# Forgetting attention: head-pair scores by full 128-row matmuls with zero-padded keys, and the decay added by VectorE

## The chip, the cores and the metric

One core of one Trainium2 chip runs the whole program. The metric is device microseconds (us) of one execution, the median of several runs. The engines are named as in the profile: PE (TensorE matmul), PEld (TensorE weight load), DVE (VectorE), ACT (ScalarE), POOL (GpSimd) and SP (SyncE, which issues all DMAs of this kernel). Each engine works through its own instructions in order and waits at semaphores for the others.

## The reference, cut to what matters

A decoder trunk of two layers on 256 tokens of width 1024 (`D_MODEL`), in float32. Layer 0 has a forgetting-attention (FoX) mixer with 16 heads of width 64, layer 1 a latent-attention mixer; each layer also has two SwiGLU half steps and a gated per-layer embedding, with a LayerNorm after each. The change is in the FoX mixer alone:

```python
def fox_mixer(x, w_in, b_f, w_o):
    # logit[t,s] = q_t.k_s/sqrt(d) + sum_{s<j<=t} log f_j
    h = x @ w_in                       # q | k | v | forget-gate logits
    ...
    cum = jnp.cumsum(jax.nn.log_sigmoid(f_logit), axis=1).transpose(0, 2, 1)
    scale = FOX_HEAD_DIM ** -0.5
    def scores(start):                 # 128 queries from start on
        ...
        s = jnp.einsum('bhqd,bkhd->bhqk', qb, k).astype(jnp.float32) * scale
        return s + cb[:, :, :, None] - cum[:, :, None, :]
    o = causal_block_attention(scores, v)   # causal mask, softmax, times v
    return o.reshape(B, S, D_MODEL) @ w_o
```

The term `cb` is the same for all keys of a query, so the softmax doesn't depend on it.

## The kernel before

Every float32 operand of a matmul is split into a high and a low part (`parts`: ACT copies the high part, DVE subtracts it for the low part), and a product is three matmuls: high x high, high x low, low x high (`mm3`). Weights stream in by SP's queue into three raw buffers; `Stream` splits each into high and low (line 163 or 171 on ACT, 164 or 175 on DVE) in one of its slots. When a split is put into the program is decided by a planner, from the durations that `S.busy(...)` and `self.mm` declare; PE's order is the program's order.

The FoX mixer (`fox`) runs: `V` (values of both token blocks), with the forget gates between (`gates`; its small steps s1 to s6 are taken from the queue `bg`, one at each use of a weight and at two places in `ws`), then a loop over eight pairs of heads, j = 0 to 7. In the loop PE does, in this order: `gen_k(j+1)` (24 matmuls of 256 columns), `T(j-1)` (six transposes of the probabilities of the pair before), `QK(j)` (scores of this pair), `gen_q(j+1)` (24 matmuls), `AV(j-1)` (three matmuls of 512 and three of 256 columns). `softmax(j)` stands behind `QK(j)`: DVE adds the causal mask and finds the maximum of each row (line 957), two small operations on each head take the query's own decay out of and back into the row's offset (lines 964 and 965), ACT takes the exponential and its sum (969), DVE the reciprocal (976), and POOL multiplies (979). A pair's probabilities are first needed in the next round of the loop, by `T`.

A pair's 128 rows of `qk` hold two heads of 64 rows. `QK` therefore works with 64 rows at a time: for each head one matmul of 384 columns adds the keys' decay (`negc`, the cumulated log gates times -8 in three parts, chosen by the selector `sel`), and six matmuls of 128 or 256 columns add the product, 14 matmuls for a pair. `gates_transpose` (two transposes by PE and a copy) makes `cq`, the decay by query, just ahead of `QK(0)`.

Of the kernel before, what the change touches and what calls it, by code (L numbers as in the profile page):

```python
# [381 lines left out]
class Trunk:  # L382
    def __init__(self, nc, pools, a, S, rec):
        self.nc, self.a, self.S = nc, a, S
        self.sb, self.ps = pools
        self.rec = rec
        self.bg = deque()
        self.setup()
# [418 lines left out]
    def fox(self, li):  # L807
# [27 lines left out]
        sel = self.tl([128, 16], F32R, "sel", 1)  # L835
        negc = self.tl([128, 384], F32R, "negc", 1)
        cq = self.tl([128, 16, 2], F32, "cq", 1)
# [5 lines left out]
        nc.gpsimd.memset(negc.bitcast(F32), 0.0)  # L843
        sf = fs[:, 1792:1808]
        nc.gpsimd.tensor_tensor(sf, self.ident[:, 16:32], self.ident[:, 48:64], op=ALU.add)
        nc.gpsimd.tensor_tensor(sf, sf, self.ident[:, 80:96], op=ALU.add)
        nc.gpsimd.tensor_tensor(sel, sf, self.ident[:, 112:128], op=ALU.add)
# [5 lines left out]
        def gates():  # L853
# [26 lines left out]
            def s4():  # L880
                nc.scalar.activation(negc[fr, 0:128], m8[:, 0:128], AF.Copy)
                nc.scalar.activation(negc[fr, 128:384], m8, AF.Copy)

            def s5():
                nc.vector.tensor_tensor(
                    negc[64:96, 128:384], m8, negc[fr, 128:384].bitcast(F32), op=ALU.subtract
                )
                nc.vector.tensor_copy(negc[64:96, 0:128], negc[64:96, 128:256].bitcast(F32))
                self.S.busy(dve=400)

            def s6():
                nc.vector.tensor_copy(negc[0:64, :], negc[64:128, :].bitcast(F32))

            rest = lambda: None
            self.bg.extend((s1, rest, rest, s2, rest, rest, s3, rest, s4, s5, s6))

        def gates_transpose():
            tr = self.bank("tr")
            for t in range(2):
                self.transpose(tr[:, 128 * t : 128 * t + 128], sc[:, 128 * t : 128 * t + 128])  # L900
            nc.vector.tensor_copy(
                cq.rearrange("p h t -> p t h"),
                tr[:, 0:256].rearrange("p (t c) -> p t c", c=128)[:, :, 112:128],
            )
# [8 lines left out]
        qk = self.own([128, 2, 2, 512], F32R, "qk")  # L913
        OT = [self.own([128, 4, 2, 256], F32R, tag) for tag in ("ota", "otb")]

        def gen(j, key, c0, at={}, hold=False):
# [534 lines left out]
```

## Time and profile before

| | |
|---|---|
| time before, median of 3 runs | 1101.17 us (1100.28 to 1101.95) |
| span of the profiled execution, first to last instruction | 1100.3 us |
| PE busy (matmul) | 1080.1 us, 98% of the span |
| DVE busy | 711.5 us, 65% |
| ACT busy | 542.5 us, 49% |
| POOL busy | 79.7 us, 7% |
| instructions | 17702 |

The profiled execution has no time of its own in the record beside its span; the span is as long as the fastest of the three runs. Matmuls overlap each other, so the busy time of one matmul is longer than the time until the next one starts: what a group of matmuls costs is read from the start of its first to the start of the next group. In a timeline each row is: start, time, engine, line, operation, what it writes and reads, shapes, count, and in brackets the idle time of the engine before it with what ended it.

### The profile page before, as it was taken

Reading aid. Unit: us, or ns where it says so; the run is one execution under the profiler, and the core shown is the slowest. Engines: PE = TensorE matmul, PEld = TensorE weight load, DVE = VectorE, ACT = ScalarE, POOL = GpSimd, SP = SyncE. Lnnn points to the kernel's source line nnn. Section 1 sums busy time; section 2 is a strip of 40 time slices with the busy share of each in tenths; the row PEclk is TensorE's granted clock in tenths of the full one; section 3 lists DMA queues with packets and bytes.
Section 4 is the critical chain, followed back from the end, with each engine's and each line's share of the span. In section 5 each row is a group of like instructions: output and inputs, shape, how many; then the busy total and the mean of one; then the engine's idle time right before and its main releaser. Section 6 shows DMA issues by size and latency. Waiting matters only on the chain. (4 is left out here: it accounts for less than half of the span.)

```text
span 1100.3 us, 17702 instructions
## 1 busy us (share of the span) xinstructions
PE 1080.1 (98%) x7186; PEld 976.7 (89%) x7186; DVE 711.5 (65%) x1006; ACT 542.5 (49%) x790; POOL 79.7 (7%) x130
## 2 busy tenths in 40 slices
PE   9999999999999999999999999998999999999997
PEld 6989998899879899997899999987899789898986
DVE  5765545788896555458975453487766885454576
ACT  5554433567645534434655353345655474445421
POOL 0000000313100000001320000011111000000000
PEclk9999999999999999999999999999999999999998
DMA  8896652553458756445677564353533678555502
GB/s 280 282 294 223 214 185 72 162 165 135 145 170 279 253 198 191 154 163 163 187 259 245 190 193 143 104 150 107 162 111 111 215 245 276 177 187 175 182 8 77
DMA packets 150676, 199.00 MB, mean 181 GB/s; under 512 B 11842, under 2 KB 128578, under 8 KB 150596
## 3 DMA queue, kind: packets, MB, share of 16 engines
q1 hardware_dynamic: 150596, 197.88, 55.6%
q8 instruction: 56, 0.92, 0.3%
q14 instruction: 24, 0.20, 0.1%
HBM read 196.81 MB, written 1.05 MB: 180 GB/s over the span
## 5 line engine op out<-in xcount | busy, mean ns | idle before, releaser
L164 DVE TENSOR_TENSOR hl<-raw,hl 128x1024 fp32r<-128x1024 f32 (+3 forms) x287 | 334.5, 1184 | 172.5 <-ACT hl L163 171.7
L163 ACT ACTIVATE hl<-raw 128x1024 fp32r<-128x1024 f32 (+3 forms) x287 | 286.9, 1021 | 198.6 <-PE y L469 82.2
L469 PE MATMUL h<-xT,hl 128*128 128x256 f32 x2016 | 239.9, 278 | 1.7 <-DVE P L613 0.7
L469 PEld LDWEIGHTS h<-xT,hl 128*128 128x128 f32 x2016 | 234.1, 188 | 3.7 <-DVE P L613 0.9
L469 PE MATMUL y<-hl,g 128*128 128x512 f32 x816 | 189.6, 390 | 0.0
L469 PEld LDWEIGHTS y<-hl,g 128*128 128x128 f32 x816 | 152.2, 188 | 31.0
L469 PE MATMUL tr<-xT,hl 128*128 128x256 f32 x864 | 102.0, 277 | 0.0
L469 PEld LDWEIGHTS tr<-xT,hl 128*128 128x128 f32 x864 | 100.0, 188 | 0.1
L469 PE MATMUL h<-hl,xT 128*128 128x512 f32 (+1 forms) x396 | 94.7, 388 | 0.4 <-DVE hl L164 0.3
L469 PEld LDWEIGHTS h<-hl,xT 128*128 128x128 f32 x396 | 72.1, 188 | 17.1 <-DVE hl L164 2.2
L541 POOL TENSOR_TENSOR rs<-ve,mhalf 128x1 f32<-128x1 f32 x16 | 15.2, 951 | 827.1 <-DVE ve L540 827.1
L469 PE MATMUL y<-hl,xT 128*128 128x512 f32 (+2 forms) x312 | 61.0, 351 | 0.0
L469 PEld LDWEIGHTS y<-hl,xT 128*128 128x128 f32 x312 | 50.8, 188 | 7.9 <-issue 0.7
L478 ACT ACTIVATE xT<-tr 128x512 fp32r<-128x512 f32 x36 | 20.2, 597 | 58.9 <-PE tr L473 58.9
L479 DVE TENSOR_TENSOR g<-P,g 128x512 fp32r<-128x512 f32 x36 | 24.9, 693 | 34.5 <-ACT g L478 34.5
L478 ACT ACTIVATE g<-P 128x512 fp32r<-128x512 f32 x36 | 22.8, 634 | 40.3 <-DVE P L648 29.4
L164 DVE TENSOR_TENSOR otb<-raw,otb 128x1024 fp32r<-128x1024 f32 (+1 forms) x20 | 24.1, 1203 | 18.9 <-ACT otb L163 18.9
L469 PE MATMUL y<-hl,ota 128*128 128x512 f32 x144 | 36.0, 393 | 0.0
L164 DVE TENSOR_TENSOR qk<-raw,qk 128x1024 fp32r<-128x1024 f32 x21 | 25.8, 1230 | 14.4 <-ACT qk L163 14.4
L469 PE MATMUL tr<-xT,qk 128*128 128x256 f32 x264 | 31.9, 277 | 0.0
L479 DVE TENSOR_TENSOR xT<-tr,xT 128x512 fp32r<-128x512 f32 x36 | 23.3, 683 | 13.3 <-ACT xT L478 13.3
L469 PEld LDWEIGHTS tr<-xT,qk 128*128 128x128 f32 x264 | 30.9, 188 | 0.0
(232 smaller groups left out, 1371.0 us busy)
## 6 DMA issues: line engine op xcount, KB each, us to landing
raw<-in_ffn_w_in_dram SPq DMA_DIRECT2D x172, 512.0 KB, 4.9
raw<-in_ffn_w_out_dram SPq DMA_DIRECT2D x44, 1024.0 KB, 5.1
raw<-in_fox_w_in_dram SPq DMA_DIRECT2D x12, 1024.0 KB, 5.3
raw<-in_ple_w_gate_dram SPq DMA_DIRECT2D x8, 1024.0 KB, 5.0
raw<-in_mla_w_o_dram SPq DMA_DIRECT2D x8, 1024.0 KB, 6.0
gb<-in_ln_g_dram SPq DMA_DIRECT2D x8, 512.0 KB, 6.3
gb<-in_ln_b_dram SPq DMA_DIRECT2D x8, 512.0 KB, 7.4
raw<-in_fox_w_o_dram SPq DMA_DIRECT2D x4, 1024.0 KB, 5.1
```

Of the source, the lines that this page charges most:

```text
L163: nc.scalar.activation(hi[:, c], src[:, c], AF.Copy)
L164: nc.vector.tensor_tensor(lo[:, c], src[:, c], hi[:, c].bitcast(F32), op=ALU.subtract)
L469: self.nc.tensor.matmul(out, lhsT, rhs, start=start, stop=stop)
L478: self.nc.scalar.activation(hi, src, AF.Copy)
L479: self.nc.vector.tensor_tensor(lo, src, hi.bitcast(F32), op=ALU.subtract)
L541: nc.gpsimd.tensor_tensor(rs, ve, self.mhalf, op=ALU.pow)
```

## The change

The scores of a pair become six matmuls over all 128 rows. The keys are kept twice as wide, in `kz`: columns 0 to 255 hold the first head's keys in rows 0 to 63 and zeros below, columns 256 to 511 the second head's in rows 64 to 127 and zeros above, so that a product with the pair's 128 rows of queries (`qq`) gives one head in each half. One bank holds both heads' scores of the first 128 queries (3 matmuls of 2 x 128 columns), the other those of the last 128 (3 of 512 columns). The zeros are written once by POOL.

The decay is no longer added by PE: step s4 stores the 16 rows of `m8` into a DRAM tile, and `load_bias(j)` loads the pair's two rows back, spread over 128 partitions, by two DMAs on SP's queue (128 x 2 x 128 and 128 x 2 x 256 elements); `mask_bias(j)` cuts the causal mask into them on POOL. DVE's line-957 operation then adds `bias` instead of `mask`. `sel`, `negc`, `cq`, `gates_transpose`, steps s5 and s6 and the two small operations on `tt` go. `gen_k` writes its high and low parts in two halves of 64 rows. One reciprocal serves both heads, and the deferred split (`S.later`) stands ahead of it.

```diff
@@ -832,19 +832,17 @@
 
         fs = self.own([128, 2048], F32, "fs")
         bf = self.tl([128, 1], F32, "bf", 1)
-        sel = self.tl([128, 16], F32R, "sel", 1)
-        negc = self.tl([128, 384], F32R, "negc", 1)
-        cq = self.tl([128, 16, 2], F32, "cq", 1)
+        bias = self.tl([128, 2, 2, 384], F32, "fbias", 1)
+        decay = self.dram.tile([16, 256], F32, name="decay")
+        kz = self.own([128, 2, 2, 512], F32R, "qk")
+        qq = self.tl([128, 2, 2, 256], F32R, "qq", 1)
         fr = slice(96, 128)
         nc.gpsimd.memset(bf, 0.0)
         if not self.rec:
             self.dma(bf[112:128, :], a["fox_b_f"][0].rearrange("(p o) -> p o", o=1))
         nc.gpsimd.memset(fs, 0.0)
-        nc.gpsimd.memset(negc.bitcast(F32), 0.0)
-        sf = fs[:, 1792:1808]
-        nc.gpsimd.tensor_tensor(sf, self.ident[:, 16:32], self.ident[:, 48:64], op=ALU.add)
-        nc.gpsimd.tensor_tensor(sf, sf, self.ident[:, 80:96], op=ALU.add)
-        nc.gpsimd.tensor_tensor(sel, sf, self.ident[:, 112:128], op=ALU.add)
+        nc.gpsimd.memset(kz[64:128, :, :, 0:256].bitcast(F32), 0.0)
+        nc.gpsimd.memset(kz[0:64, :, :, 256:512].bitcast(F32), 0.0)
 
         f, e, u, r, ab = (fs[fr, 256 * i : 256 * i + 256] for i in range(5))
         sc = fs[:, 1280:1536]
@@ -878,30 +876,29 @@
                 self.S.busy(dve=600)
 
             def s4():
-                nc.scalar.activation(negc[fr, 0:128], m8[:, 0:128], AF.Copy)
-                nc.scalar.activation(negc[fr, 128:384], m8, AF.Copy)
-
-            def s5():
-                nc.vector.tensor_tensor(
-                    negc[64:96, 128:384], m8, negc[fr, 128:384].bitcast(F32), op=ALU.subtract
-                )
-                nc.vector.tensor_copy(negc[64:96, 0:128], negc[64:96, 128:256].bitcast(F32))
-                self.S.busy(dve=400)
-
-            def s6():
-                nc.vector.tensor_copy(negc[0:64, :], negc[64:128, :].bitcast(F32))
+                self.dma(decay, m8[16:32, :])
+                for j in range(2):
+                    load_bias(j)
+                mask_bias(0)
 
             rest = lambda: None
-            self.bg.extend((s1, rest, rest, s2, rest, rest, s3, rest, s4, s5, s6))
-
-        def gates_transpose():
-            tr = self.bank("tr")
-            for t in range(2):
-                self.transpose(tr[:, 128 * t : 128 * t + 128], sc[:, 128 * t : 128 * t + 128])
-            nc.vector.tensor_copy(
-                cq.rearrange("p h t -> p t h"),
-                tr[:, 0:256].rearrange("p (t c) -> p t c", c=128)[:, :, 112:128],
-            )
+            self.bg.extend((s1, rest, rest, s2, rest, rest, s3, s4))
+
+        def load_bias(j):
+            b = bias[:, j % 2]
+            for c0, w in ((0, 128), (128, 256)):
+                if not self.rec:
+                    d = decay[2 * j : 2 * j + 2, 0:w]
+                    src = bass.AP(tensor=d.tensor, offset=d.offset, ap=[[0, 128], [256, 2], [1, w]])
+                    self.dma(b[:, :, c0 : c0 + w], src)
+
+        def mask_bias(j):
+            b = bias[:, j % 2]
+            for c0 in (0, 256):
+                nc.gpsimd.affine_select(
+                    out=b[:, :, c0 : c0 + 128], in_=b[:, :, c0 : c0 + 128],
+                    pattern=[[0, 2], [-1, 128]], compare_op=ALU.is_ge, fill=NEG, base=0, channel_multiplier=1,
+                )
 
         V(0, 0)
         V(1, 0, VAT, lambda: self.XT(1))
@@ -910,79 +907,73 @@
         V(1, 1)
 
         st, PT = {}, {}
-        qk = self.own([128, 2, 2, 512], F32R, "qk")
         OT = [self.own([128, 4, 2, 256], F32R, tag) for tag in ("ota", "otb")]
 
-        def gen(j, key, c0, at={}, hold=False):
+        def gen_k(j):
             ps = self.bank("h")
-            ws((key, j), ps[:, 0:256], at, hold)
-            o = qk[:, j % 2]
-            self.parts(o[:, 0, c0 : c0 + 256], o[:, 1, c0 : c0 + 256], ps[:, 0:256])
-
-        def gen_k(j):
-            gen(j, "fk", 256, {0: S.split_now} if j >= 2 else {}, j >= 2)
+            ws(("fk", j), ps[:, 0:256], {0: S.split_now} if j >= 2 else {}, j >= 2)
+            o = kz[:, j % 2]
+            part = [(slice(64 * s, 64 * s + 64), slice(256 * s, 256 * s + 256)) for s in range(2)]
+            for r, c in part:
+                nc.scalar.activation(o[r, 0, c], ps[r, 0:256], AF.Copy)
+            for r, c in part:
+                nc.vector.tensor_tensor(o[r, 1, c], ps[r, 0:256], o[r, 0, c].bitcast(F32), op=ALU.subtract)
+            self.S.busy(act=600, dve=600)
 
         def gen_q(j):
-            gen(j, "fq", 0, {}, j >= 2)
+            ps = self.bank("h")
+            ws(("fq", j), ps[:, 0:256], {}, j >= 2)
+            o = qq[:, j % 2]
+            self.parts(o[:, 0, :], o[:, 1, :], ps[:, 0:256])
 
         def QK(j, ring):
             sb = [self.bank(ring) for _ in range(2)]
-            half = [slice(0, 64), slice(64, 128)]
-            o = qk[:, j % 2]
-            for s in range(2):
-                h = 2 * j + s
+            q, k = qq[:, j % 2], kz[:, j % 2]
+            pairs = lambda ap: ap.rearrange("p (s c) -> p s c", s=2)
+            for n, (i, jj) in enumerate(((0, 0), (0, 1), (1, 0))):
                 self.mm(
-                    sb[s][:, 0:384], sel[half[s], h : h + 1].to_broadcast([64, 128]), negc[half[s], :],
-                    True, False,
+                    pairs(sb[0][:, 0:256]), q[:, i, 0:128], pairs(k[:, jj])[:, :, 0:128], n == 0, n == 2
                 )
             for n, (i, jj) in enumerate(((0, 0), (0, 1), (1, 0))):
-                for q0, c0, c1 in ((0, 0, 128), (128, 128, 384)):
-                    for s in range(2):
-                        self.mm(
-                            sb[s][:, c0:c1], o[half[s], i, q0 : q0 + 128],
-                            o[half[s], jj, 256 : 256 + c1 - c0], False, n == 2 and q0 > 0,
-                        )
+                self.mm(sb[1], q[:, i, 128:256], k[:, jj], n == 0, n == 2)
             st[j] = sb
 
         def softmax(j):
             sb = st[j]
             nm = self.tl([128, 4], F32, "nm", 2)
-            tt = self.tl([128, 4], F32, "tt", 2)
             su = self.tl([128, 4], F32, "su", 2)
             pair = self.tl([128, 768], F32, "P", 2)
             P = [pair[:, 384 * s : 384 * s + 384] for s in range(2)]
             seg = ((0, 128), (128, 384))
+            S2 = [[sb[q][:, w * s : w * s + w] for q, w in enumerate((128, 256))] for s in range(2)]
             for s in range(2):
                 for q, (c0, c1) in enumerate(seg):
                     nc.vector.tensor_tensor_reduce(
-                        out=sb[s][:, c0:c1], in0=sb[s][:, c0:c1], in1=self.mask[:, c0:c1],
+                        out=S2[s][q], in0=S2[s][q], in1=bias[:, j % 2, s, c0:c1],
                         op0=ALU.add, op1=ALU.min, scale=-0.125, scalar=3.0e38,
                         accum_out=nm[:, 2 * s + q : 2 * s + q + 1],
                     )
-                c2 = cq[:, 2 * j + s, :]
-                i = slice(2 * s, 2 * s + 2)
-                nc.vector.tensor_tensor(tt[:, i], nm[:, i], c2, op=ALU.subtract)
-                nc.vector.tensor_tensor(tt[:, i], tt[:, i], c2, op=ALU.add)
+            if j < 6:
+                load_bias(j + 2)
             for s in range(2):
                 for q, (c0, c1) in enumerate(seg):
                     i = 2 * s + q
                     nc.scalar.activation(
-                        P[s][:, c0:c1], sb[s][:, c0:c1], AF.Exp, bias=tt[:, i : i + 1], scale=-1.0,
+                        P[s][:, c0:c1], S2[s][q], AF.Exp, bias=nm[:, i : i + 1], scale=-1.0,
                         accum_out=su[:, i : i + 1],
                     )
             self.S.busy(act=1800, dve=1400)
 
-            def divide(s):
-                nc.vector.reciprocal(su[:, 2 * s : 2 * s + 2], su[:, 2 * s : 2 * s + 2])
+            S.later()
+            nc.vector.reciprocal(su, su)
+            for s in range(2):
                 for q, (c0, c1) in enumerate(seg):
                     i = 2 * s + q
                     nc.gpsimd.tensor_scalar(
                         P[s][:, c0:c1], P[s][:, c0:c1], su[:, i : i + 1], 1.0, op0=ALU.mult, op1=ALU.mult
                     )
-
-            divide(0)
-            divide(1)
-            S.later()
+            if j < 7:
+                mask_bias(j + 1)
             st[j] = P
 
         def T(j):
@@ -1049,7 +1040,6 @@
                 O(1, 0)
             if j == 0:
                 self.flush()
-                gates_transpose()
                 S.lend("fs")
             if j >= 1:
                 T(j - 1)
@@ -1434,7 +1425,7 @@
     from concourse import mybir as _mybir
     from concourse.bass_utils import run_bass_kernel_spmd as _run
 
-    nc = _bacc.Bacc("TRN2", target_bir_lowering=False, num_devices=1)
+    nc = _bacc.Bacc("TRN2", target_bir_lowering=False, num_devices=1, dynamic_dma_scratch_size=1024)
     arrays, aps = {}, {}
     given = {n: _np.ascontiguousarray(inputs[n]) for n in _INS}
     given["rope"] = _rope_tables(_np)
```

## Rows read from the trace of the kernel before

**Rows 1.** The page, engines: busy us (share of the span), instructions.
```profile
PE 1080.1 (98%) x7186; PEld 976.7 (89%) x7186; DVE 711.5 (65%) x1006; ACT 542.5 (49%) x790; POOL 79.7 (7%) x130
```
**Rows 2.** One round by windows: us, busy (count) of each, granted clock, DMA share, GB/s.
```profile
252.00:260.50 8.50, 8.50 (x77) 8.07 (x76) 7.29 (x23) 5.97 (x17) 2.56 (x4) 1.00 0.39 131
```
**Rows 3.** Timeline of PE: AV(2), gen_k(5), T(3), QK(4), start of gen_q(5).
```profile
255.84 1.21 PE L469 MATMUL y<-PT,g 128*128 128x512 f32 x6
256.89 3.00 PE L469 MATMUL h<-xT,hl 128*128 128x256 f32 x24
...
259.73 0.60 PE L994 MATMUL tr<-ident,P 128*128 128x128 f32 x4
260.16 0.38 PE L473 MATMUL tr<-ident,P 128*128 128x128 f32 x2
260.47 0.44 PE L469 MATMUL y<-negc,sel 64*128 64x384 f32 x2
...
261.53 0.63 PE L469 MATMUL h<-xT,hl 128*128 128x256 f32 x3
```
**Rows 4.** Timeline of PE: gen_k(1), gates_transpose, QK(0), T(0).
```profile
224.31 3.01 PE L469 MATMUL h<-xT,hl 128*128 128x256 f32 x24 [0.62 <-DVE qk L479]
227.16 0.38 PE L473 MATMUL tr<-ident,fs 128*128 128x128 f32 x2
227.47 0.44 PE L469 MATMUL y<-negc,sel 64*128 64x384 f32 x2
...
234.10 0.60 PE L994 MATMUL tr<-ident,P 128*128 128x128 f32 x4
```
**Rows 5.** Timeline of the other engines and SP around pair 0.
```profile
219.60 1.44 POOL L877 TENSOR_SCALAR fs<-fs 32x256 f32<-32x256 f32 x1 [1.08 <-DVE fs L876]
...
222.13 0.37 SPq L323 DMA_DIRECT2D raw<-in_fox_w_in_dram  x1
...
222.74 0.42 DVE L885 TENSOR_TENSOR negc<-fs,negc 32x256 fp32r<-32x256 f32 x1
...
223.83 0.42 DVE L479 TENSOR_TENSOR qk<-h,qk 128x256 fp32r<-128x256 f32 x1
...
228.63 0.30 DVE L957 CUSTOM_DVE_ANT_0 y<-y,mask 128x128 f32<-128x128 f32 x1 [0.34 <-PE y L469]
...
232.56 1.64 POOL L979 TENSOR_SCALAR P<-P,su 128x128 f32<-128x128 f32 x4 [11.53 <-DVE su L976]
```
**Rows 6.** Timeline of DVE and POOL: softmax(3).
```profile
253.54 0.29 DVE L957 CUSTOM_DVE_ANT_0 y<-y,mask 128x128 f32<-128x128 f32 x1
...
255.93 0.17 DVE L976 RECIPROCAL su<-su 128x2 f32<-128x2 f32 x1
...
257.03 0.17 DVE L976 RECIPROCAL su<-su 128x2 f32<-128x2 f32 x1 [0.93 <-ACT P L969]
257.11 1.20 DVE L175 TENSOR_TENSOR hl<-raw,hl 128x1024 fp32r<-128x1024 f32 x1
...
257.29 1.73 POOL L979 TENSOR_SCALAR P<-P,su 128x128 f32<-128x128 f32 x2 [0.26 <-DVE su L976]
```
**Rows 7.** DMA issues, whole run: count, KB each, median us from issue to landing.
```profile
gb<-in_ln_b_dram SPq DMA_DIRECT2D x8, 512.0 KB, 7.4
...
raw<-in_kv_w_up_dram SPq DMA_DIRECT2D x8, 256.0 KB, 3.4
...
out_dram<-x SPq DMA_DIRECT2D x4, 256.0 KB, 2.0
```
**Rows 8.** Timeline of POOL: the mask at the start, and the gates.
```profile
4.19 0.54 POOL L441 TENSOR_SCALAR_AFFINE_SELECT mask<-mask 128x128 f32<-128x128 f32 x2 [2.51 <-PE y L452]
...
211.18 0.41 POOL L862 TENSOR_SCALAR fs<-fs 32x256 f32<-32x256 f32 x1 [9.96 <-ACT fs L860]
```
**Rows 9.** DVE groups by line and form, 200 to 300 us: busy us, mean ns.
```profile
L1023 DVE TENSOR_TENSOR ota<-y,ota 64x256 fp32r<-64x256 f32 x8 | 3.3, 417 | 0.1
...
L964 DVE TENSOR_TENSOR tt<-nm,cq 128x2 f32<-128x2 f32 x16 | 2.6, 160 | 0.5
```

More of the change, by code (lines that the diff above doesn't have):

```diff
@@ L384, in __init__ @@
         self.nc, self.a, self.S = nc, a, S
-        self.sb, self.ps = pools
+        self.sb, self.ps, self.dram = pools
         self.rec = rec
@@ L880, in s4 @@
             def s4():
-                nc.scalar.activation(negc[fr, 0:128], m8[:, 0:128], AF.Copy)
-                nc.scalar.activation(negc[fr, 128:384], m8, AF.Copy)
-            def s5():
-                nc.vector.tensor_tensor(
-                    negc[64:96, 128:384], m8, negc[fr, 128:384].bitcast(F32), op=ALU.subtract
-                )
-                nc.vector.tensor_copy(negc[64:96, 0:128], negc[64:96, 128:256].bitcast(F32))
-                self.S.busy(dve=400)
-            def s6():
-                nc.vector.tensor_copy(negc[0:64, :], negc[64:128, :].bitcast(F32))
-            rest = lambda: None
-            self.bg.extend((s1, rest, rest, s2, rest, rest, s3, rest, s4, s5, s6))
-        def gates_transpose():
-            tr = self.bank("tr")
-            for t in range(2):
-                self.transpose(tr[:, 128 * t : 128 * t + 128], sc[:, 128 * t : 128 * t + 128])
-            nc.vector.tensor_copy(
-                cq.rearrange("p h t -> p t h"),
-                tr[:, 0:256].rearrange("p (t c) -> p t c", c=128)[:, :, 112:128],
-            )
+                self.dma(decay, m8[16:32, :])
+                for j in range(2):
+                    load_bias(j)
+                mask_bias(0)
+            rest = lambda: None
+            self.bg.extend((s1, rest, rest, s2, rest, rest, s3, s4))
[12 more added lines that the diff above has]
+                    pattern=[[0, 2], [-1, 128]], compare_op=ALU.is_ge, fill=NEG, base=0, channel_multiplier=1,
+                )
         V(0, 0)
@@ L1402, in tile_trunk @@
     ps = ctx.enter_context(tc.tile_pool(name="ps", bufs=1, space=bass.MemoryType.PSUM))
+    dr = ctx.enter_context(tc.tile_pool(name="dr", bufs=1, space=bass.MemoryType.DRAM))
     ctx.enter_context(tc.manual_schedule())
@@ L1408, in tile_trunk @@
     d = Dummy()
-    Trunk(d, (d, d), d, r, True).run()
+    Trunk(d, (d, d, d), d, r, True).run()
     S = Stream(nc, raw, sb, make_loads(a), r.seq)
-    Trunk(nc, (sb, ps), a, S, False).run()
+    Trunk(nc, (sb, ps, dr), a, S, False).run()
 _INS = [
```

## Prediction

> **What bounds the kernel now.** I read the page first: PE is busy for 98% of the span, every other engine for 65% or less [rows 1]. Busy time of overlapping matmuls says little by itself, so I looked at the windows of the FoX loop: in a round of 8.5 us PE has no gap, DVE is busy 7.29 us, ACT 5.97, POOL 2.56, the DMA engines have a share of 0.39, and the granted clock is 1.00, the 2.4 GHz level [rows 2]. So a round lasts as long as PE's own list, and what the change is worth there is the issue time of the matmuls that it removes and adds, as long as nothing else becomes late. Third came the timeline of PE in one round, for the time from the start of one group to the start of the next [rows 3], and last the stretch ahead of pair 0, where PE stands still for 0.62 us before gen_k(1) [rows 4].
>
> **QK, each pair.** Before, the 14 matmuls take from 260.47 to 261.53, 1.06 us [rows 3]. They are entered with a gap: four transposes take 0.43 us (259.73 to 260.16), 0.108 each, but the last two take 0.31 until QK starts, where two are worth 0.215; 0.095 us is lost at the step from 128 to 64 rows [rows 3]. After, QK is three matmuls of 512 columns and three of 2 x 128 columns with 128 rows. AV is exactly that mixture, strided blocks included, and takes from 255.84 to 256.89, 1.05 us, with no gap ahead [rows 3]. So a pair gains 0.01 + 0.095 = 0.105 us; pairs 1 to 7 gain 0.74. Bounds: no gain, if the gap belongs to QK and not to the change of rows; 0.2 us a pair if shorter weight traffic (6 loads for 14) helps too.
>
> A rule speaks against this edit: the Trainium skill, TensorEngine Tiling (Array Packing), When to Use Tiling, wants row tiling for 64 rows of contraction, since two tiles run side by side; the change gives this up. The rows show why little is lost: AV's 2304 columns take 1.05 us, and at that rate the 1536 paired columns of before would take 0.70, but they take 1.06 [rows 3]. By the rule alone the sum would have 0.35 us a pair on the other side. The same page's Key Properties says that a change of the tiling mode drains TensorE, with which the 0.095 us agree.
>
> **The stretch ahead of pair 0.** PE waits 0.62 us for the low part of gen_k(0), which frees a bank [rows 4]. DVE does it only at 223.83, because steps s5 and s6 stand ahead of it from 222.74 on [rows 5]. Without them two halves of 0.42 us (the 64-row form takes 417 ns too [rows 9]) end at 223.58, before PE is done with gen_q(0) at 224.31 - 0.62 = 223.69. The wait goes: 0.62 us. The two transposes and the gap, 227.16 to 227.47, go: 0.31 [rows 4]. With its own 0.01, QK(0) ends 0.94 us earlier, at 227.59.
>
> **The new chain of pair 0.** `m8` is ready at 219.60 + 1.44 = 221.04 [rows 5]; s4 is taken from the queue one use earlier than before, so SP's order is: store, four loads, then the weight load that before went at 222.13 [rows 5]. None of this was in the trace, so I bound it. Store: 2.0 us, the only store there is [rows 7]; the loads wait for it. Then an issue of 0.37 us [rows 5] and the second load, 256 KB: 3.4 us by the load of the same size, 7.4 by the row that is also spread from one DRAM row over 128 partitions, but is twice as large and stands behind others [rows 7]. Then two selects on POOL: 0.27 us for 128 elements [rows 8], so 0.54 each; the first lies beside the second load. Best case: 221.04 + 2.0 + 0.37 + 3.4 + 0.54 = 227.35, before DVE could start on QK(0) anyway (227.59 + 0.1 = 227.7). Worst: 231.35, or 233.1 if both selects are held by DVE as below. I take 228.6, nearer to the load of the same size.
>
> From the start of line 957 to the end of POOL's four multiplications it was 228.63 to 234.20, 5.57 us [rows 5]. Two small operations ahead of the first exponential go (0.16 each [rows 9]), while POOL now waits for all four exponentials; I keep 5.57. Probabilities are then ready at 234.2. PE would come to T(0) at 234.10 - 0.94 = 233.16 and need the last of them three transposes later, at 233.5 [rows 4]. PE waits 0.7 us. A start of line 957 up to 227.9 costs nothing, 229.6 eats all of 1.68 us that the rest gains, 231.8 makes the kernel slower by 0.2%. Behind the waiting operation on DVE stand the reciprocal and gen_q(1)'s low part, which PE needs only at QK(1). The weight load that SP delays by some 3 us feeds splits of a later round, since loads run three groups ahead.
>
> **What is hidden.** gen_k's second half costs ACT and DVE about 0.4 us a pair more; four operations on `tt` (0.64 us) and one reciprocal leave DVE, which also waited 0.93 us for ACT in each round [rows 6, 9]. But DVE's line 957 starts later by that half, at 253.94 for 253.54. Its four operations with `tt` took 2.39 us, until 255.93 [rows 6]; without the 0.64 us they end at 255.69. Then the deferred split, 1.20, the reciprocal 0.17 with 0.1 to POOL, and four multiplications, 1.64 [rows 5, 6]: 258.8. Before, POOL was done at 259.02 [rows 6]; T reads from 259.73 on [rows 3]. So no wait, with 0.9 us of cover; if that is gone, PE waits the rest once in each round. The next selects follow on POOL, 1.1 us, up to 259.9, or 261.7 if both are held; line 957 of the next round starts at about 262.4. The zeros of `kz` are written by POOL, which idles 9.96 us ahead of 211.18 [rows 8]. Loads for later pairs, 384 KB a round, go into a queue with a share of 0.39 [rows 2], issued a whole round ahead.
>
> The two multiplications beside DVE's line 175 took 1.73 us, four without it 1.64 [rows 5, 6]: 0.9 us for one that meets it. The Trainium skill, GPSIMD Engine Reference, Specifications, says that its SBUF interfaces are shared with VectorE and contend with instructions of two SBUF inputs, which line 175 is; the trace agrees. The new place of the split takes it out of the multiplications' way in the loop; in pair 0 they may still meet (0.9 us, in the bounds).
>
> The planner is told other durations (fewer columns, more for gen_k), so behind the loop a split may move by one place: up to its 1.20 us of DVE [rows 6] either way, taken as nothing.
>
> **Sum.** -0.94 - 0.74 + 0.7 = -1.0 us. Against the profiled span of 1100.3 that is 1099.3; the median of the runs lies 0.9 above the span, and the time is 1101.17 - 1.0 = **1100.2 us**.
>
> **The rivals.**
> *The decay arrives late.* With 7.4 us for the load, line 957 starts at 231.35, probabilities are ready at 236.9, PE waits 3.4 us and the kernel takes 1101.17 - 1.68 + 3.4 = 1102.9; with held selects 1104.6. For it: store and load follow each other on one queue, and nothing here shows a load that must wait for a store. Against it: no other load is in flight then. It decides from a start at 229.6 (no gain) or 231.8 (slower).
> *The softmax's chain gets too long in every round.* If the split ahead of the reciprocal waits for ACT, or multiplications meet another split, the cover of 0.9 us is overrun. Twice 0.9 us leaves 0.9 of wait in each of seven rounds: 1100.2 + 6.3 = 1106.5; once, nothing. Against it: DVE's idle 0.93 us [rows 6].
> *Row tiling was worth more.* If the 64-row matmuls of two heads cost no more than their paired columns, 0.70 us, and the rest of the 1.06 is a wait at the entry and exit of QK that stays, then QK with full rows takes 0.35 us a pair more than before: 1101.17 + 8 x 0.35 - 0.93 = 1103.0. For it: 1536 columns at AV's rate. Against it: AV, entered in the same way, shows no such wait [rows 3]. (This is what the page's advice on 64-row contractions would lead to.)
> *Nothing on PE's path.* The step from 128 to 64 rows is no gap that goes, and pair 0's lead is lost to its new chain: 1101.2.
>
> **How the numbers follow.** Forecast 0.52 (own range 1099.4 to 1101.4), late decay 0.20, a longer chain in every round 0.10, row tiling 0.05, nothing on the path 0.13. The likeliest gives 1100.2. A measurement tells 0.2%, 2.2 us, from no change. Faster than 1098.97 needs more than all the gains that I can count (1.68 us), so also a lucky place of splits: 0.10, out of the forecast's chance. Slower than 1103.37: half of the late decay, 0.07 of the longer chain, 0.03 of row tiling: 0.20. The same: 0.70. The range goes from 1098.8 (all gains, and some 0.7 from splits) to 1104.0, past most of the late decay; about 0.09 is left out on each side.
>
> **What would show it.** In the trace after: QK's six matmuls take 1.05 us from start to start, with no gap behind the transposes; no PE idle ahead of gen_k(1); the store and loads of pair 0 land by 228, and PE's idle at T(0) is under 1.5 us; no PE wait on POOL in later rounds. The prediction is wrong if PE's idle at T(0) is over 3 us, if T waits in every round, or if QK with full rows takes more than 1.2 us.

## The result and the profile after

The changed kernel takes **1103.78 us** (median of 9 runs, 1102.91 to 1105.21) against 1101.17 in the same session (9 runs, 1100.28 to 1102.05): a ratio of 1.0026, 95% interval [1.0017, 1.0035]. It is slower by 2.6 us where 1.0 us less was forecast; the interval does not reach 1, but its lower end, 1.9 us, is below the 2.2 us that the prediction took as the least that a measurement can tell. The span of the profiled execution went from 1100.3 to 1103.2 us. In every execution on record that has both, the time is 1.7 to 1.9 us longer than the span; the 0.9 us that the prediction put between the two compares different executions. It does no harm there, as only differences were used, but both profiled executions are slower than the median of their kernel, by about 0.9 us before and 1.2 us after.

Busy shares tell nothing of it; PE is again busy for 98%, now with 66 matmuls fewer. The page of the kernel after, engines:

```profile
PE 1082.5 (98%) x7120; PEld 980.9 (89%) x7120; DVE 708.3 (64%) x970; ACT 543.5 (49%) x796; POOL 86.7 (8%) x144
```

PE's timeline around pair 0, after (its counterpart is [rows 4]):

```profile
218.35 8.54 PE L469 MATMUL h<-xT,hl 128*128 128x256 f32 x72
226.74 1.21 PE L469 MATMUL y<-qk,qq 128*128 128x256 f32 x6
227.79 5.61 PE L469 MATMUL h<-xT,hl 128*128 128x256 f32 x48
235.51 1.28 PE L985 MATMUL tr<-ident,P 128*128 128x128 f32 x3 [2.11 <-POOL P L972]
237.72 0.47 PE L985 MATMUL tr<-ident,P 128*128 128x128 f32 x1 [0.94 <-POOL P L972]
237.99 0.64 PE L473 MATMUL tr<-ident,P 128*128 128x128 f32 x2
238.28 2.27 PE L469 MATMUL y<-qk,qq 128*128 128x256 f32 x6
240.34 4.13 PE L469 MATMUL h<-xT,hl 128*128 128x256 f32 x24
244.31 1.21 PE L469 MATMUL y<-PT,g 128*128 128x512 f32 x6
```

Three things are to be seen. The 0.62 us stall is gone: 72 matmuls run through, and QK(0) starts 0.73 us earlier (226.74 for 227.47). At T(0), PE waits for POOL, 2.11 us ahead of the first transpose and 0.94 us more between the first three and the last. And from there on PE itself is slow: QK(1), 1.05 us in pair 0, takes 2.06 (238.28 to 240.34), and gen_q(2), 2.8 elsewhere, takes 3.97. The windows of the kernel after say why (us; busy and count of PE, PEld, DVE, ACT, POOL; granted clock; DMA share; GB/s):

```profile
228.00:233.40 5.40, 5.40 (x48) 5.20 (x46) 2.10 (x10) 1.64 (x3) 0.82 (x2) 1.00 0.98 328
233.40:236.40 3.00, 0.76 (x3) 0.37 (x3) 0.99 (x3) 2.98 (x12) 1.32 (x4) 0.95 1.08 338
236.40:242.40 6.00, 5.06 (x20) 4.48 (x21) 4.69 (x14) 2.94 (x9) 1.99 (x3) 0.50 0.15 45
```

PE is busy without a gap until 233.4, for only 0.76 of the next 3.0 us, and then the granted clock is 0.50, the 1.2 GHz level, for 6.0 us. From 233.40 to 237.99, when T(0)'s last two transposes start, PE is idle for 3.2 us.

The span splits at two events that both traces have, the starts of QK(0) and of the AVs. Ahead of QK(0): -0.73. From QK(0) to AV(0): 11.29 us before (227.47 to 238.76), 17.57 after, **+6.28**. From AV(0) to AV(7): 58.36 before (to 297.12), 57.06 after (to 301.37), **-1.30**. From there to the end: 803.18 before, 801.83 after, -1.35. The sum is the +2.9 us of the spans. The change does pay wherever nobody waits; the loss lies in one stretch, of pair 0 alone.

What pair 0 waits for is in the other engines' timelines after (counterparts in [rows 5]; for SP the second column is the time over which it issues):

```profile
219.89 1.44 POOL L875 TENSOR_SCALAR fs<-fs 32x256 f32<-32x256 f32 x1 [1.08 <-DVE fs L874]
...
221.35 0.33 SPq L404 DMA_DIRECT2D decay<-fs  x1
223.32 1.90 SPq L404 DMA_DIRECT2D fbias<-decay  x4
...
228.41 0.41 POOL L898 TENSOR_SCALAR_AFFINE_SELECT fbias<-fbias 128x256 f32<-128x256 f32 x1 [7.08 <-DMA fbias<-decay]
230.49 0.41 POOL L898 TENSOR_SCALAR_AFFINE_SELECT fbias<-fbias 128x256 f32<-128x256 f32 x1 [1.67 <-DMA fbias<-decay]
...
230.93 0.43 DVE L951 CUSTOM_DVE_ANT_0 y<-y,fbias 128x256 f32<-128x256 f32 x1 [1.67 <-POOL fbias L898]
...
231.75 1.28 ACT L961 ACT_TABLE_LOAD   x1 [4.03 <-DVE nm L951]
...
234.79 0.18 DVE L968 RECIPROCAL su<-su 128x4 f32<-128x4 f32 x1 [2.74 <-ACT P L961]
...
235.07 2.59 POOL L972 TENSOR_SCALAR P<-P,su 128x128 f32<-128x128 f32 x4 [4.18 <-DVE su L968]
...
236.01 1.31 DVE L175 TENSOR_TENSOR hl<-raw,hl 128x1024 fp32r<-128x1024 f32 x1 [0.52 <-ACT hl L171]
```

The selects wait for the DMA, DVE's second operation for the second select, ACT's table load for DVE, the one reciprocal for all four exponentials, and the four multiplications take 2.59 us where they took 1.64 before [rows 5], because line 175 starts in the middle of them. The table load is not new. The kernel before has it too, ahead of its first exponential (and DVE's second operation at 229.02):

```profile
229.02 0.43 DVE L957 CUSTOM_DVE_ANT_0 y<-y,mask 128x256 f32<-128x256 f32 x1
...
229.98 1.28 ACT L969 ACT_TABLE_LOAD   x1 [2.24 <-DVE tt L965]
```

So it is part of the chain, and of the 5.57 us that the prediction kept, but not of what the change made longer. The DMA issues of the whole run give the time to landing of the loads that the selects wait for (count, KB each, median us to landing):

```profile
fbias<-decay SPq DMA_DIRECT2D x8, 256.0 KB, 6.9
...
fbias<-decay SPq DMA_DIRECT2D x8, 128.0 KB, 5.2
...
decay<-fs SPq DMA_DIRECT2D x1, 16.0 KB, 2.0
```

In later rounds PE does not wait. PE's timeline after, AV(1) to gen_q(4) (counterpart [rows 3]), and the windows of that round (counterpart [rows 2]):

```profile
252.74 1.23 PE L469 MATMUL y<-PT,g 128*128 128x512 f32 x6
253.81 2.89 PE L469 MATMUL h<-xT,hl 128*128 128x256 f32 x24
256.54 0.60 PE L985 MATMUL tr<-ident,P 128*128 128x128 f32 x4
256.97 0.38 PE L473 MATMUL tr<-ident,P 128*128 128x128 f32 x2
257.11 1.29 PE L469 MATMUL y<-qk,qq 128*128 128x256 f32 x6
258.24 2.89 PE L469 MATMUL h<-xT,hl 128*128 128x256 f32 x24
```

```profile
252.70:261.20 8.50, 8.50 (x70) 8.20 (x70) 7.25 (x19) 6.51 (x19) 3.33 (x6) 1.00 0.74 171
```

From the last two transposes to gen_q it is 1.27 us (256.97 to 258.24), 1.37 before [rows 3]. Rounds last 8.22 to 8.43 us, 8.32 in the mean of AV(0) to AV(5), where they lasted 8.54.

### The profile page after: what moved, and what is told of

It is laid out like the page before. It is cut to its first block, busy times and chain, and to the rows that moved or that the text cites. A ratio compares the mean times of both kernels' runs of the same rounds, so it can differ in the third digit from the quotient of the medians.

```text
span 1103.2 us, 17622 instructions
## 1 busy us (share of the span) xinstructions
PE 1082.5 (98%) x7120; PEld 980.9 (89%) x7120; DVE 708.3 (64%) x970; ACT 543.5 (49%) x796; POOL 86.7 (8%) x144
```

## The experiments

The theory ahead of the first four runs: pair 0's decay arrives late, and PE's idle then brings the slow clock. The run without a load showed that more stands in the way, and from the fifth run on the theory (A) is: the loss is pair 0's chain from `m8` to its probabilities, late by three delays in a row (slow loads, the table load, held multiplications), plus the slow clock that PE's idle brings. The rivals are named in the expectations. Line numbers in the text are those of the kernel after; where a run adds lines, its rows show the same operation some lines lower. Each kernel is compared with the kernel before on the same chip: 1101.39 us for the first four (33 runs), 1101.62 for the next four (35 runs), 1101.56 for the last two (23 runs).

**No load for pair 0.** Its bias is set to zero at the start and then masked as before; pair 0's decay is left out.

```diff
 def s4():
     self.dma(decay, m8[16:32, :])
-    for j in range(2):
-        load_bias(j)
+    load_bias(1)
     mask_bias(0)
...
+nc.gpsimd.memset(bias[:, 0], 0.0)
```

> Pair 0's decay is left out of the computation: its bias is set to zero by POOL at the start of the mixer and only masked, nothing is loaded for it. Theory (pair 0's decay arrives late, and PE's idle at T(0) then costs its clock): PE does not idle at T(0), the clock stays at 1.00, and the time is 1103.8 - 4.2 (wait) - 2.3 (half clock from 236.4 to 242.1) = about 1097.3 us, below the kernel before. Rival (the full-row scores, the second half of gen_k or the loads of every round cost the time): at most 1 us is gained, 1102.8 us or more.

Measured: 1100.81 us (1097.84 to 1102.97, 11 runs), ratio 0.9992 [0.9984, 1.0001]. The profiled execution was the shortest, and in it PE still waits. Its timelines of ACT and POOL, and of PE:

```profile
229.35 1.28 ACT L961 ACT_TABLE_LOAD   x1 [2.06 <-DVE nm L951]
...
232.69 2.60 POOL L972 TENSOR_SCALAR P<-P,su 128x128 f32<-128x128 f32 x4 [10.16 <-DVE su L968]
```

```profile
233.12 1.14 PE L985 MATMUL tr<-ident,P 128*128 128x128 f32 x3
235.34 0.33 PE L985 MATMUL tr<-ident,P 128*128 128x128 f32 x1 [1.09 <-POOL P L972]
```

With no load at all the loss is gone, 3.0 us less than after, but the 1097.3 expected was missed by 3.5 us: line 951 starts at 228.21, the probabilities are ready at 235.29, 7.08 us later, and the last transpose of the first four waits for them. So the wait for the load is a large delay and not the only one. That the profiled execution is 2.5 us shorter than the next of this kernel says little of pair 0: it takes 787.4 us from the wait on line 546, behind the mixer, to the end, where all other profiles but one take 789.3 to 790.4.

**Pair 0's loads alone on the queue.** Pair 1's are issued only in softmax(0).

```diff
-    for j in range(2):
-        load_bias(j)
+    load_bias(0)
...
+            if j == 0:
+                load_bias(1)
             if j < 6:
                 load_bias(j + 2)
```

> Only pair 0's two loads follow the store; pair 1's are issued in softmax(0), behind the weight loads. If pair 0's loads are late because pair 1's stand on the same queue with them, the second load lands 4 us after its issue instead of 6.7, line 951 of pair 0 is done 2.5 us earlier and the time falls to about 1099 to 1101 us. If the spread from one DRAM row is slow by itself, it still lands 6 us or more after its issue, and the time stays within 1 us of 1103.8.

Measured: 1104.43 us, ratio 1.0021 [1.0011, 1.0030], as slow as after. The loads land about as late as in the kernel after (5.2 and 6.9 us):

```profile
fbias<-decay SPq DMA_DIRECT2D x8, 256.0 KB, 6.5
...
fbias<-decay SPq DMA_DIRECT2D x8, 128.0 KB, 5.0
```

PE waits 2.44 and 1.09 us at T(0), and the granted clock falls to 0.50 again. Loads of pair 1 on the same queue are not what makes pair 0's slow.

**Eight copies of the decay.** The store writes each row eight times; partition p reads copy p mod 8, one head per load.

```diff
-decay = self.dram.tile([16, 256], F32, name="decay")
+decay = self.dram.tile([16, 8, 256], F32, name="decay")
-self.dma(decay, m8[16:32, :])
+self.dma(decay, m8[16:32, None, :].to_broadcast([16, 8, 256]))
...
-    d = decay[2 * j : 2 * j + 2, 0:w]
-    src = bass.AP(tensor=d.tensor, offset=d.offset, ap=[[0, 128], [256, 2], [1, w]])
-    self.dma(b[:, :, c0 : c0 + w], src)
+    for h in range(2):
+        d = decay[2 * j + h, :, 0:w]
+        src = bass.AP(tensor=d.tensor, offset=d.offset, ap=[[0, 16], [256, 8], [1, w]])
+        self.dma(b[:, h, c0 : c0 + w], src)
```

> The store writes eight copies of the decay (128 KB instead of 16), and each partition loads from copy p mod 8; a load goes for each head by itself, so four loads a pair instead of two. If reading the same DRAM row 128 times is what makes the loads slow (90 GB/s at a DMA share of 0.3), they run at 200 GB/s or more, the last of pair 0 lands by 228 instead of 230.5, and the time falls by 2 to 6 us. If the size of the pieces (512 and 1024 bytes) is what makes them slow, nothing gets faster, and two more issues and a larger store make it 1 us slower.

Measured: 1103.80 us, ratio 1.0011 [1.0001, 1.0021], in two clusters: four runs at 1100.35 to 1100.72, seven at 1103.64 to 1105.03, and one between. The DMA issues of this kernel:

```profile
fbias<-decay SPq DMA_DIRECT2D x16, 128.0 KB, 2.6
...
fbias<-decay SPq DMA_DIRECT2D x16, 64.0 KB, 2.2
...
decay<-fs SPq DMA_DIRECT2D x1, 128.0 KB, 3.2
```

And its timeline of SP and POOL:

```profile
224.17 5.78 SPq L404 DMA_DIRECT2D fbias<-decay  x8
...
228.71 0.41 POOL L899 TENSOR_SCALAR_AFFINE_SELECT fbias<-fbias 128x256 f32<-128x256 f32 x1 [1.13 <-DMA fbias<-decay]
```

128 KB land in 2.6 us in place of 5.2. These are not the same loads, since each now holds one head, but pair 0's 384 KB as a whole take 4.54 us from the first issue to the second select (224.17 to 228.71), where after takes 7.17 (223.32 to 230.49), with pieces of the same sizes. So bytes and pieces are not what makes the loads slow, and that all 128 partitions read the same row is the likely cause. The run also splits each load by head, and the weight loads go out behind all eight (230.04 for 225.32). No run tells these apart for pair 0; the medians, which are over all pairs, fall too. The larger store takes part of it back (3.2 us for 2.0): from the store's issue to the second select it is 7.8 us (220.94 to 228.71) for 9.1 after. The fall of 2 to 6 us that was expected is not in the median; by the ratios the kernel gains 1.6 us on after. In the profiled execution (1100.35 us) PE idles 0.74 and 1.09 us at T(0): table load, four exponentials, and 2.60 us of held multiplications still stand behind it.

**PE kept busy.** 36 transposes of the identity ahead of T(0), in pair 0 alone; the wait stays, PE works through it.

```diff
 b0, b1 = self.bank("tr"), self.bank("tr")
+for _ in range(36 if j == 0 else 0):
+    nc.tensor.transpose(b0[:, 0:128], self.ident, self.ident)
```

> 36 needless transposes of the identity (3.9 us at 0.108) stand ahead of T(0) on PE, nothing else is changed. If the fall of the clock is a consequence of PE's idle and costs 2.3 us, the clock stays at 1.00 through pair 1 and the kernel gets faster by 2 us, to about 1101.6, with more work on PE. If the clock has another cause or costs nothing, the time stays at 1103.8 or grows.

Measured: 1103.09 us (1102.23 to 1104.04), ratio 1.0013 [1.0004, 1.0021]. The windows of this kernel, where after had 0.76 and 0.82 for the clock:

```profile
232.00:240.00 8.00, 8.00 (x70) 7.74 (x70) 4.18 (x10) 6.18 (x16) 3.32 (x6) 1.00 0.65 207
240.00:248.00 8.00, 8.00 (x66) 7.74 (x65) 5.88 (x15) 5.99 (x17) 2.35 (x6) 1.00 0.42 155
```

T(0) starts later (237.11 for 235.51), but with no idle there is no fall, QK(1) takes 1.13 us, and AV(0) starts at 241.76 for 244.31. With more work on PE AV(0) comes 2.5 us earlier in the profiles; by the ratios (1.0013 for 1.0026, with intervals that overlap) the kernel is 1.4 us faster than after, less than the 2 us expected. The mean granted clock of its eleven executions is 0.997 to 0.999, that of the nine of after 0.993 to 0.997. So the idle brings the fall of the clock, and the fall costs a second time. The Trainium skill, TensorE: Matmul & The Clock Gate, Part 1, says that an idle PE is put at 1.2 GHz and that sustained work releases it; the 0.50 of after, and its absence here, agree.

**The table loaded early.** One exponential of a 128x1 zero right behind the gates' logarithm.

```diff
+warm = self.tl([128, 1], F32, "warm", 1)
+nc.gpsimd.memset(warm, 0.0)
...
 def s3():
+    nc.scalar.activation(warm, warm, AF.Exp)
...
```

> ACT loads the table for the exponential right after the gates' logarithm (one exponential of a 128x1 zero) and no longer between line 951 and the first exponential of pair 0. Theory A (the lost time is the chain of pair 0 from the arrival of its decay to its probabilities, plus the slower clock that PE's idle brings with it): the 1.28 us of the load leave the chain, so PE's idle at T(0) falls from about 4.2 to 2.9 us and the median from 1103.8 to about 1102.5, or to about 1100 if the shorter idle no longer pulls the granted clock down. Rival B (the lost time lies outside of pair 0: QK with full rows, or a longer softmax in every round): no change, 1103.8.

Measured: 1102.57 us, ratio 1.0013 [1.0004, 1.0022]. In the profile no table load stands behind line 951:

```profile
231.69 0.37 ACT L964 ACTIVATE P<-y,nm 128x128 f32<-128x128 f32 x1 [4.20 <-DVE nm L954]
```

The first exponential starts 1.35 us earlier than after (233.04), PE waits 1.02 and 1.09 us, and the median is the 1102.5 that theory A gave. It does not make the table load a cause of the loss, since the kernel before has it too; it shows that a shorter chain of pair 0 shortens the kernel. The runs (1100.51 to 1104.70) still spread as if the clock fell in some.

**Copies and early table together.**

> Both shortenings together: eight copies of the decay in DRAM (loads of 2.2 to 2.6 us in place of 4.9 to 6.8), and the table loaded early. Theory A: the third line-951 operation of pair 0 ends at about 229.2, the first exponential starts there in place of 231.2 (copies alone), the division ends at about 233.9 even if line 175 still holds GpSimd for 0.9 us, and PE, which arrives at 233.1, idles at most 1 us; the clock does not fall, and the executions lie close together at 1098.0 (1097.0 to 1099.5), below the kernel before. Rival B: 1103. Rival C (the two clusters of the run with copies come from something other than PE's idle at T(0)): still two clusters.

Measured: 1102.13 us (1099.90 to 1104.16), ratio 1.0002 [0.9993, 1.0010]. The 1098.0 expected was a miss of 4 us. The second select starts at 229.12, 0.4 later than with the copies alone, and the multiplications, 232.46 to 235.06, are held in full: the last of T(0)'s first four transposes starts only at 235.11. The idle that theory A put at 1 us at most was 1.6 (QK(0) to QK(1) takes 8.92 us, 7.30 in the next run), and the spread (mean clocks from 0.994 to 0.998) suggests that one condition of the 1098.0, no fall of the clock in any execution, did not hold either.

**And pair 0's multiplications on DVE.**

```diff
-nc.gpsimd.tensor_scalar(
+(nc.vector if j == 0 else nc.gpsimd).tensor_scalar(
     P[s][:, c0:c1], P[s][:, c0:c1], su[:, i : i + 1], 1.0, op0=ALU.mult, op1=ALU.mult
 )
```

> As the run with copies and early table, and pair 0's four multiplications by the reciprocal on VectorE in place of GpSimd, so that line 175 can't hold them. Theory A: the probabilities of pair 0 are ready before PE comes to T(0) at 233.1, PE does not idle there at all, and the median is 0 to 1 us below that of the run with copies and early table: 1097.5 (1096.5 to 1098.5). If the collision with line 175 was of no weight: the same as that run within 0.3 us.

Measured: **1099.10 us** (1097.76 to 1102.16, 12 runs), ratio **0.9977 [0.9968, 0.9985]**. It is faster than both kernels, though the 1097.5 expected (1096.5 to 1098.5) was missed by 1.6 us. Its timelines of DVE and PE:

```profile
232.11 1.01 DVE L976 TENSOR_SCALAR P<-P,su 128x128 f32<-128x128 f32 x4
...
233.38 1.22 DVE L175 TENSOR_TENSOR hl<-raw,hl 128x1024 fp32r<-128x1024 f32 x1
```

```profile
232.67 0.84 PE L989 MATMUL tr<-ident,P 128*128 128x128 f32 x4
233.35 0.38 PE L473 MATMUL tr<-ident,P 128*128 128x128 f32 x2
233.48 1.30 PE L469 MATMUL y<-qk,qq 128*128 128x256 f32 x6
```

Four multiplications take 1.01 us in DVE's own order, line 175 comes after them, and T(0) starts when PE gets there. Against the run above only the engine of these four differs: 1.6 us from QK(0) to QK(1), 3.0 us in the medians. The early table load could go into the kernel before too, which was not run; PE does not wait for pair 0 there, though [rows 4].

**QK with 64 rows.** Twelve matmuls, the heads in the two halves of the rows, a bank per head; the decay stays with DVE.

```diff
...
-for n, (i, jj) in enumerate(((0, 0), (0, 1), (1, 0))):
-    self.mm(pairs(sb[0][:, 0:256]), q[:, i, 0:128], pairs(k[:, jj])[:, :, 0:128], n == 0, n == 2)
-for n, (i, jj) in enumerate(((0, 0), (0, 1), (1, 0))):
-    self.mm(sb[1], q[:, i, 128:256], k[:, jj], n == 0, n == 2)
+for n, (i, jj) in enumerate(((0, 0), (0, 1), (1, 0))):
+    for q0, c0, c1 in ((0, 0, 128), (128, 128, 384)):
+        for s in range(2):
+            self.mm(sb[s][:, c0:c1], q[half[s], i, q0 : q0 + 128],
+                    k[half[s], jj, 256 * s : 256 * s + c1 - c0], n == 0 and q0 == 0, n == 2 and q0 > 0)
...
```

> QK as twelve matmuls of 64 rows, the two heads in the two halves of the rows, each head with a bank of its own; decay still added by VectorE, no matmuls for the decay. This asks what full rows alone are worth. Theory A (at the entry and exit of a group of 64-row matmuls some 0.1 us each is lost, and their columns run no faster than full rows): the stretch from the last two transposes to gen_q stays within 0.15 us of the 1.27 us with full rows, pair 0 waits as in the kernel after, and the median is 1103.8 (1102.5 to 1104.8). Rival D (row tiling is worth 0.35 us a pair, since two heads share the array): the stretch takes 0.9 to 1.0 us, and the median is about 1101.

Measured: 1102.32 us, ratio 1.0010 [0.9999, 1.0020]. One round in PE's timeline:

```profile
243.71 0.60 PE L986 MATMUL tr<-ident,P 128*128 128x128 f32 x4
244.15 0.38 PE L473 MATMUL tr<-ident,P 128*128 128x128 f32 x2
244.46 0.95 PE L469 MATMUL y<-qk,qq 64*128 64x128 f32 x12
245.34 3.10 PE L469 MATMUL h<-xT,hl 128*128 128x256 f32 x24
```

The twelve take 0.88 us (244.46 to 245.34) where full rows take 1.13, but are entered with a gap (0.31 us from the last two transposes, 0.14 with full rows), and gen_q behind them takes up to 2.93 in place of 2.72 to 2.83. AV(0) to AV(7) is 57.44 us, 0.38 more than in after; ten profiles with full rows lie between 56.94 and 57.20. That is 0.03 to 0.07 us a pair for full rows. Rival D, 0.35 us a pair for row tiling, is out. The median is lower than after's, and just below the range expected (1102.5 to 1104.8), and its profile points to the reason. Pair 0's chain is shorter here: the first exponential waits for one head's bank alone, and in this kernel the table load stands ahead of that wait (227.41); PE reaches QK(1) at 236.09, 2.2 us earlier than after.

**Multiplications on DVE alone, and with the early table.** The loads stay those of after.

> The kernel after with one edit: pair 0's four multiplications by the reciprocal on VectorE (1.0 us for the four in the run with copies, early table and this) in place of GpSimd, where line 175 holds them (2.6 us). Loads from one DRAM row and the late table load stay. Theory A (three delays in a row on pair 0's chain, whose sizes add: slow loads, the table, the held multiplications): the probabilities are ready 1.6 us earlier, at about 236.0, PE's idle at T(0) is 2.5 us in place of 4.2, and the median is about 1102.2; executions without a fall of the clock lie near 1100.5. Rival (the multiplications only hide behind the other delays): 1103.8 as the kernel after.

> As the run with the early table load, and pair 0's multiplications on VectorE; the loads from one DRAM row stay as in the kernel after. It tells what the slow loads cost when the chain behind them is short. Theory A: the third line-951 operation ends at 231.6 as before, the probabilities are ready at about 234.6, PE's idle at T(0) is 1.1 to 1.6 us, and the median lies 1.2 to 2 us above the run with all three measures (1099.1) and at or below the kernel before: 1100.5 (1099.5 to 1101.6). If the slow loads alone decide the loss: no better than the early table load alone, 1102.6.

Measured: 1102.46 us, ratio 1.0003 [0.9995, 1.0011], for the first; **1100.16 us** (1099.11 to 1101.12, 11 runs), ratio **0.9986 [0.9978, 0.9995]**, for the second. PE's T(0) in either:

```profile
234.69 1.05 PE L985 MATMUL tr<-ident,P 128*128 128x128 f32 x4 [1.77 <-DVE P L972]
```

```profile
233.12 1.05 PE L988 MATMUL tr<-ident,P 128*128 128x128 f32 x4 [0.18 <-DVE P L975]
```

Both medians lie near those of theory A (1102.2 and 1100.5) and away from the rivals' (1103.8 and 1102.6). The waits are shorter than it had them, 1.77 us for 2.5 and 0.18 for 1.1 to 1.6; the second profile is of an execution whose second select started at 229.51, 230.49 in after. With the chain behind them short, the slow loads cost 0.44 us from QK(0) to AV(0) in the profiles, and 1.0 us by the ratios (0.9986 against 0.9977 with copies), whose intervals overlap.

Taken alone, the three measures gain by the ratios 1.6 us (copies), 1.4 (table) and 2.5 (DVE) on the kernel after, and together 5.4: within the noise they add. The multiplications, not the loads, are the largest of the three.

Laid side by side, the stretch from QK(0) to AV(0) in the profiled execution orders the kernels, but for two that differ elsewhere too (no load for pair 0, which leaves a part out, and 64 rows, whose later rounds are 0.4 us longer):

```
kernel                 QK(0) to AV(0), us   ratio to before
all three measures            11.27             0.9977
table, DVE                    11.71             0.9986
copies, table                 12.89             1.0002
no load (part left out)       13.31             0.9992
64 rows                       13.32             1.0010
DVE                           13.43             1.0003
copies                        13.89             1.0011
table                         14.17             1.0013
filled                        15.08             1.0013
loads of pair 0 alone         17.14             1.0021
after                         17.57             1.0026
```

Each stretch is of one execution, in six of these kernels the shortest of all its runs, while the ratios go by all runs. From the first row to the last the stretch grows by 6.3 us and the ratio by 0.0049, 5.4 us. At 11.27, about the 11.29 of the kernel before, PE has hardly a gap.

## Why the prediction was wrong, point by point

- **QK, each pair** (a gain of 0.105 us): the stretch from the last two transposes to gen_q gained 0.10 (1.37 to 1.27), as forecast, but by two errors that cancel, which is luck: the gap at the entry gave 0.17 (0.31 to 0.14) for 0.095, and six full-row matmuls take 1.13 where 1.05 was forecast, 0.07 more than the fourteen before. A whole round gained 0.19 us (1.30 over seven); the rest of it lies in the products beside QK (gen_k 2.73 for 2.84 in the rounds shown). By the run with 64 rows, some 0.05 of it is worth of full rows, and 0.13 comes with the rest of the change, the decay matmuls that are no longer there among it (58.36 to 57.44 us over seven rounds). The prediction had the gap at the entry right in kind and priced the dropped matmuls at almost nothing, where the twelve without them take 0.18 us less than the fourteen.
- **The stretch ahead of pair 0** (0.94 us earlier): right. The stall is gone, DVE's two halves take 0.42 us each, gen_q(1) starts at 227.79 where 227.59 was forecast, in an execution that came to this stretch 0.29 us later (218.35 for 218.06).
- **The new chain of pair 0: its load.** This is the step that failed first. The prediction took 3.4 us for the second load "nearer to the load of the same size" and put the start of line 957 (now 951) at 228.6; measured were 6.9 us, and DVE's second operation at 230.93. Of the two rows at hand the nearer one was the 7.4 us of the load that is also spread from one row [rows 7], twice as large, and not the 3.4 us of the load of the same size. The bound was in the text, and the value was taken from its other end. A start at 228.6 would have put DVE's second operation at 229.0, so the load made the chain 1.9 us late.
- **The new chain: "I keep 5.57".** The second failure. From the start of line 951 to the end of the multiplications it takes 7.08 us even without a load. In the whole chain of after, DVE's second operation to the end of the multiplications takes 6.73 us (230.93 to 237.66) and took 5.18 before (229.02 to 234.20); with the load's 1.9 this is the 3.5 us by which the probabilities missed the 234.2 of the forecast. Before, the first two of the four multiplications could begin while ACT was still at the other head's exponentials; with one reciprocal all four begin after the last one, and then meet line 175. From the table load to the start of the multiplications it is 3.34 us in the run without a load (229.35 to 232.69), 2.58 before: 0.76 us for the common wait. The collision (2.60 for 1.64 us) stood in the bounds as 0.9 us and is in every run that leaves these operations on POOL; the common wait was seen ("POOL now waits for all four exponentials") and priced at nothing.
- **PE waits 0.7 us**: QK(1) comes some 4.2 us late (QK(0) to QK(1) takes 11.54 us after and 7.30 with all three measures); 3.2 us of it show as idle. That 3 us and more would mark the prediction as wrong was said.
- **The clock** stood in no term. After that idle PE ran at 1.2 GHz for 6 us and lost about 2.1 us more: QK(1) 2.06 for 1.13, gen_q(2) 3.97 for 2.83. About two thirds of the loss between QK(0) and AV(0) is the wait and one third the clock. The "late decay" rival had the right cause, and the median of 1103.78 lies within its price of 1102.9 to 1104.6, but the number is in part luck: it had no term for the clock, its upper end was for selects held by DVE, which took 0.41 us each, and in the profiles the rest of the kernel gained 3.4 us where it counted 1.68.
- **What is hidden** held: the selects, the later loads, the zeros and the second halves of gen_k cost PE nothing in later rounds, and the rival of a longer chain in every round did not come.
- **Not in the sum:** 0.6 us between AV(7) and the layer norm's transposes, where a wait of 0.21 us on `otb` is gone; the 0.8 us further on lies within what executions of these kernels differ there (from the wait on line 546 to the end, 787.4 to 790.4 us over twelve profiles), so it can't be put down to the change.

Left open: why the runs of one kernel fall in two clusters (copies alone). It fits executions with and without a fall of the clock, since mean granted clocks were 0.998 in the four shortest and 0.994 to 0.997 in the rest, but none of the longer ones was profiled. The mean clock alone doesn't prove it: a second place, near 760 us, shows a low clock in some executions too (in the profile of after 0.65 from 764 to 768), and the shortest run of the kernel with DVE alone has 0.995. The change also sets `dynamic_dma_scratch_size`, as do all runs here; no run shows what that is worth by itself.

## What to carry to other kernels

When work moves off the bound engine to a chain of other engines, price the first pass through that chain, where nothing runs ahead, by itself: here the seven later rounds hid everything and the first gave back nearly five times what they gained (6.28 us for 1.30). Take the price of a transfer from the row with the same access pattern, not from the one with the same size. And a wait on PE of some microseconds may have to be priced twice, once as idle and once as the slow clock behind it (here 4.2 and 2.1 us). When several things stand in one chain, a load that is made faster only shows the next one: copies and early table alone left PE waiting for the multiplications.

## What the runs showed of the hardware that was not expected

- A load in which 128 partitions read the same DRAM row took 5.2 us for 128 KB and 6.9 for 256 KB; with eight copies of the row and a load for each head, 2.6 us for 128 KB. Without the next pair's loads behind it on the queue it took 5.0 and 6.5 us.
- Four multiplications on GpSimd took 1.63 us free and 2.60 us beside one VectorE operation with two SBUF inputs; two selects took 0.76 us free and 1.75 beside the same operation. In both cases GpSimd took about 1 us longer.
- Twelve 64-row matmuls in two row halves ran in 0.88 us where six full-row ones took 1.13, and gave 0.17 us of it back at the entry (0.31 us from the last two transposes, 0.14 with full rows) and up to 0.1 us in the gen_q behind them.
- On PE 3.2 us of idle within 4.6 us were followed by 6 us at half the clock; with the wait filled by 36 needless transposes the clock stayed at 1.00, and AV(0) came 2.5 us earlier.
